# Keys and values of a gated linear attention turned by VectorE in 32 by 32 blocks and gathered by DMAs, in place of TensorE transposes

## The chip, the cores and the metric

The kernel runs on one core of a Trainium2 chip. The metric is the device time of one execution in microseconds (us). Engines are named as in the profile: PE (TensorE), DVE (VectorE), ACT (ScalarE), POOL (GpSimd) and SP (SyncE), which here issues DMAs.

## What is computed

One inference step of a decoder with two layers over 320 tokens: a prompt of 256 and 8 samples of 8 new tokens each. Layer 0 mixes tokens by gated linear attention (GLA), layer 1 by a gMLP with spatial gating; each is followed by a dense MLP of 2048 to 8192 to 2048. The change lies in GLA alone. Cut to that:

```python
D_MODEL = 2048; GLA_HEADS = 4; GLA_HEAD_K = 256; GLA_HEAD_V = 512; GLA_CHUNK = 64

def gla_chunked(q, k, v, log_a, s0):              # one head: q, k (T, 256), v (T, 512)
    def step(s, inp):
        qi, ki, vi, gi = inp                      # a chunk of at most 64 tokens
        b = jnp.cumsum(gi, axis=-2)
        b_last = b[..., -1:, :]
        q_dec = qi * jnp.exp(b)
        k_inv = ki * jnp.exp(-b)
        k_to_end = ki * jnp.exp(b_last - b)
        scores = jnp.where(causal, jnp.einsum('bhtk,bhsk->bhts', q_dec, k_inv), 0.0)
        o = (jnp.einsum('bhtk,bhkv->bhtv', q_dec, s)
             + jnp.einsum('bhts,bhsv->bhtv', scores, vi))
        s_new = (jnp.exp(b_last[..., 0, :])[..., None] * s
                 + jnp.einsum('bhsk,bhsv->bhkv', k_to_end, vi))
        return s_new, o

def gla_mixer(x, w_in, w_gate, b_gate, norm_g, w_out, s0):
    q, k, v, r, g_low = split(x @ w_in)
    log_a = log_sigmoid(g_low @ w_gate + b_gate) / 16
    o, s_fin = gla_chunked(q, k, v, log_a, s0)
    o = o * rsqrt(mean(o * o) + 1e-6) * norm_g    # per head
    return (o * silu(r)) @ w_out, s_fin
```

The prompt starts from a zero state, each sample from a state of its own that is loaded from memory and written back.

## The kernel before

**Tokens lie along the free axis.** A projection leaves features on the 128 partitions and the 320 tokens in the columns (0 to 255 prompt, 256 to 319 samples). Scores are computed from that layout. Three products need keys or values with tokens on the partitions instead: the outputs from the scores (`prompt_o`, `sample_first`), the prompt's final state (`prompt_state`) and the samples' state updates (`sample_step`). So keys and values are turned: `ev_k` and `ev_v`, called as the projection of 128 key or value features ends, do it.

**Weights.** Every weight matrix is cut into units of 512 rows and 256 columns. `unit()` has SP load one into `raw` (L138, 512 KB, three buffers), ACT cast it to a rounded high part `wh` (L144) and DVE subtract to get the low part `wl` (L145); `wh` and `wl` have four buffers each until `second_half()`, a second set after it. TensorE multiplies a unit in 24 matmuls: for each of 4 blocks of rows and 2 of columns wl by x_high, wh by x_low, wh by x_high (L161 to L163). `group()` runs 4 units for 256 output columns, or 8 for two such blocks that share the inputs, and then calls the evictions. Units are counted here in the order in which TensorE uses them: head 0 uses units 1 to 8 for V, 9 to 16 for K and Q, 17 to 24 for the gate R; heads 1 to 3 use, from 24h + 1 on, 8 for K and Q, 8 for V (two groups of 4) and 8 for R. The output projection `gla_w_out` starts at unit 97.

**Side work.** A `Side` object holds a list of steps and runs some of them after each unit: gates of the next head, and the attention steps of a head (`Head.steps`) during its R units and the next head's K, Q units. The steps are written in program order, but the order on each engine is set when the program is built, by a scheduler with its own estimate of when inputs are ready; so an instruction may stand far from where it was written. An engine then runs its list strictly in order. SP's list holds the loads of weights and of sample states (`load`, L578), and each DMA of it uses one of eight completion counters in turn, so that a DMA waits for the one eight places before.

**The turn before.** `ev_k` prepares two tiles of 128 features by 256: `kend` (prompt) and `kst` (samples, 32 columns for each, high and low part), `ev_v` likewise `vfm` and `vst`. Each is transposed on TensorE in two blocks of 128 by 128 into PSUM (L420, L422, L456, L458) and copied from there by ACT or DVE: to `ktp` (L424), `kz` (L429, L431: each sample's keys alone, zeros around them), `vtp` (L460), `vts` (L461).

**Buffers.** Pool `g3` has four buffers of 512 KB under the tag "st", in which the states of the samples and the prompt's new state turn; `gp` has one buffer to a tag, `g2` two. `gltile()` gives one of four PSUM tiles. At the end of a head `sample_o` turns the samples' outputs back (L615), sums squares over features by a matmul with ones (L625), and `rsqrt` (L186 to L190) makes the norm's factor.

Of the kernel before, what the change touches and what calls it, by code (L numbers as in the profile page):

```python
# [8 lines left out]
F32 = mybir.dt.float32  # L9
F32R = mybir.dt.float32r  # L10
# [5 lines left out]
P = 128  # L16
# [61 lines left out]
def step_kernel(ctx: ExitStack, tc: tile.TileContext, A):  # L78
# [3 lines left out]
    def nm(s):  # L82
        uid[0] += 1
        return f"{s}_{uid[0]}"
# [22 lines left out]
    def gltile(n=512):  # L107
        return gl.tile([P, n], F32, tag="gl", name=nm("gl"), padded_shape=[P, 512])
# [173 lines left out]

    kz = gp.tile([P, 2, 4, DK], F32R, tag="kz", name="kz")
    nc.gpsimd.memset(kz[:].bitcast(F32), 0.0)
# [6 lines left out]
    def load_gates():  # L291

        nc.sync.dma_start(wgr, A["gla_w_low"])
        wgr2 = gp.tile([P, 2, DV], F32, tag="vtp", name="wgr2")[:].rearrange("p a b -> p (a b)")
        for i in range(6):
            nc.sync.dma_start(wgr2[16 * i : 16 * (i + 1), :], A["gla_w_gate"])
        nc.scalar.copy(wg2[:], wgr2[0:96])
        nc.vector.tensor_sub(wg2[64:96, :], wgr2[64:96], wg2[64:96, :].bitcast(F32))
# [25 lines left out]
    def bc4(ap):  # L324

        return ap.rearrange("p (b o t) -> p b o t", b=DB, o=1)

    def chunks(ap):
        return ap.rearrange("p (n w) -> p n w", w=CH)

    class Head:
# [58 lines left out]
        def factors(hd):  # L390
# [6 lines left out]
            nc.vector.tensor_mul(fac[:, :, 5:6], fac[:, :, 2:3], d3)  # L397

        def ev_k(hd, kt, ps):
            ei, ee = hd.ei[kt], hd.ee[kt]  # L400
# [15 lines left out]
            nc.vector.tensor_sub(kst[:, :, 2:4, :], bc4(kte[:, TP:T]).to_broadcast(two), hi)  # L416
            pt = gltile()
            ks = kst[:].rearrange("p b c t -> p (b c t)")
            for blk in range(2):
                nc.tensor.transpose(pt[:, blk * P : (blk + 1) * P], kend[:, blk * P : (blk + 1) * P], ident[:])  # L420
            for g in range(2):
                nc.tensor.transpose(pt[:, TP + g * P : TP + (g + 1) * P], ks[:, g * P : (g + 1) * P], ident[:])  # L422
            cs = slice(kt * P, (kt + 1) * P)
            nc.scalar.copy(hd.ktp[:, :, cs], pt[:, 0:TP].rearrange("p (b f) -> p b f", f=P))  # L424
            for i in range(4):
                rows = slice(32 * i, 32 * (i + 1))
                src = pt[rows, TP:].rearrange("p (b f) -> p b f", f=P)
                if i % 2:
                    nc.scalar.copy(kz[rows, :, i, cs], src)  # L429
                else:  # L430
                    nc.vector.tensor_copy(kz[rows, :, i, cs], src)  # L431

# [12 lines left out]
        def ev_v(hd, vt, ps):  # L445
            vfm = g2.tile([P, TP], F32, tag="vfm", name=nm("vfm"))
            nc.scalar.copy(vfm[:], ps[:, 0:TP])
            vst = g2.tile([P, DB, 4, DS], F32, tag="vst", name=nm("vst"))
            two = [P, DB, 2, DS]
            hi = vst[:, :, 0::2, :]  # L450
            nc.scalar.copy(hi.bitcast(F32R), bc4(ps[:, TP:T]).to_broadcast(two))
            nc.vector.tensor_sub(vst[:, :, 1::2, :], bc4(ps[:, TP:T]).to_broadcast(two), hi)
            pt = gltile()
            vs = vst[:].rearrange("p b c t -> p (b c t)")
            for blk in range(2):
                nc.tensor.transpose(pt[:, blk * P : (blk + 1) * P], vfm[:, blk * P : (blk + 1) * P], ident[:])  # L456
            for g in range(2):
                nc.tensor.transpose(pt[:, TP + g * P : TP + (g + 1) * P], vs[:, g * P : (g + 1) * P], ident[:])  # L458
            cs = slice(vt * P, (vt + 1) * P)
            nc.scalar.copy(hd.vtp[:, :, cs], pt[:, 0:TP].rearrange("p (b f) -> p b f", f=P))  # L460
            nc.vector.tensor_copy(hd.vts[:, :, cs], pt[:, TP:].rearrange("p (b f) -> p b f", f=P))  # L461

# [70 lines left out]
        def prompt_o(hd, i):  # L533
# [6 lines left out]
            for v in range(2):  # L540
                vs = slice((2 * i + v) * P, (2 * i + v + 1) * P)
                nc.tensor.matmul(pv[:, v, :], hd.vtp[:, 0, vs], scp[:, 0:W0], start=(v == 0), stop=False)  # L542
                nc.tensor.matmul(pv[:, v, P:TP], hd.vtp[:, 1, vs], scp[:, W0:], start=False, stop=(v == 1))  # L543
            nc.scalar.copy(o_all[:, 4 * h + 2 * i : 4 * h + 2 * i + 2, 0:TP], pv)
# [8 lines left out]
        def prompt_state(hd, kt):  # L553
            if kt == 0:
                hd.S = g3.tile([P, 2, DV], F32, tag="st", name=nm("S"))
            pu = gltile()
            for blk in range(2):
                nc.tensor.matmul(pu[:], hd.ktp[:, blk, kt * P : (kt + 1) * P], hd.vtp[:, blk, :],  # L558
                                 start=(blk == 0), stop=(blk == 1))
# [20 lines left out]
        def sample_first(hd):  # L580

            hd.st = {}
            hd.load(0)
            hd.load(1)
            hd.po = gltile()
            for g in range(2):
                nc.tensor.matmul(hd.po[:], scst[:, g, :], hd.vts[:, g, :], start=(g == 0), stop=False)

        def sample_step(hd, b, kt):
# [12 lines left out]
            pu = gltile()  # L602
            nc.tensor.matmul(pu[:], kz[:, g, i, kt * P : (kt + 1) * P], hd.vts[:, g, :], start=True, stop=True)  # L603
            nc.vector.scalar_tensor_tensor(st[:, kt, :], st[:, kt, :], hd.dec[:, kt, NCH + b : NCH + b + 1],
# [500 lines left out]
```

## Time and profile before

| | |
|---|---|
| median of 3 runs | 2703.79 us (2703.7 to 2705.22) |
| the profiled execution | 2703.75 us |
| its span in the profile | 2702.0 us |
| mean granted TensorE clock | 0.999 |
| PE, DVE, ACT, POOL busy | 2692.4, 1543.5, 1182.8, 53.5 us |
| DMA | 434.53 MB, mean 161 GB/s |

The profile shows one execution. Its span runs from the first to the last instruction, and the time of the execution is 1.75 us longer. A busy time is the union of an engine's instructions; matmuls overlap, so the sum of their durations is more than what they take of the span. Line numbers are those of each kernel's own file: a line of the kernel before that lies behind the change stands 16 to 19 lines further down in the changed one (L600 becomes L616, L615 L631, L625 L641; L569 and L521 become L588 and L537).

### The profile page before, as it was taken

The page shows a single profiled execution, that of the slowest core. Times are in us where ns is not written, and L with a number is a line of the kernel's source. Part 1 is how long each engine was busy: PE and PEld are TensorE (multiplying, and loading weights), DVE is VectorE, ACT ScalarE, POOL GpSimd, SP SyncE. Part 2 cuts the span into 40 slices and gives each one's busy share as a digit, 9 for nine tenths or more (in the row PEclk, how much of TensorE's full clock was granted, in tenths as well). Part 3 has the DMA queues.
Part 4 walks back from the last instruction along what each step waited for, and adds up shares of the span by engine and source line. Part 5 has one row for each costly group of instructions (what it writes and reads, how often), then busy time and mean ns, then how long its engine had stood idle before and what let it go on. Part 6 is the DMA issues. An engine that isn't in the chain of part 4 may idle for free.

```text
span 2702.0 us, 44679 instructions
## 1 busy us (share of the span) xinstructions
PE 2692.4 (100%) x18515; PEld 2669.7 (99%) x18515; DVE 1543.5 (57%) x2289; ACT 1182.8 (44%) x1702; POOL 53.5 (2%) x83
## 2 busy tenths in 40 slices
PE   9999999999999999999999999999999999999998
PEld 9999999999999999999999999999999999999998
DVE  6667577885444444444468775587444444444456
ACT  6545455464234334333445554355334323333434
POOL 1000001000000000000001000000000000000000
PEclk9999999999999999999999999999999999999999
DMA  7656556644445455444445444454444545554442
GB/s 243 193 188 228 185 190 218 211 146 156 152 151 154 151 154 151 153 151 153 150 148 171 150 140 136 140 162 155 150 155 150 154 151 153 152 153 152 153 152 79
DMA packets 126396, 434.53 MB, mean 161 GB/s; under 512 B 13680, under 2 KB 17904, under 8 KB 126192
## 3 DMA queue, kind: packets, MB, share of 16 engines
q1 hardware_dynamic: 119136, 407.82, 48.6%
q0 software_dynamic: 6512, 23.20, 2.6%
q8 instruction: 145, 2.38, 0.4%
q10 hardware_dynamic: 544, 0.66, 0.1%
q14 instruction: 59, 0.48, 0.1%
HBM read 409.60 MB, written 22.02 MB: 160 GB/s over the span
## 4 chain that ended last, share of the span: by engine, by line
PE 99%; ACT 0%; DMA 0%; DVE 0%; issue 0%; ACTq 0%; DVEq 0%
PE mm L161 32%; PE mm L163 31%; PE mm L162 31%; PE gl L600 1%; PE gl L603 1%; PE gl L558 1%; PE gl L948 0%; PE gl L542 0%; DMA raw<-gla_w_in 0%; ACT z L1038 0%; PE gl L943 0%; DMA xr<-xT 0%; PE gl L543 0%; PE gl L458 0%; PE gl L456 0%; PE gl L521 0%
## 5 line engine op out<-in xcount | busy, mean ns | idle before, releaser
L145 DVE TENSOR_TENSOR wl<-raw,wh 128x1024 fp32r<-128x1024 f32 (+1 forms) x740 | 901.6, 1219 | 938.8 <-ACT wh L144 936.3
L144 ACT CAST wh<-raw 128x1024 fp32r<-128x1024 f32 (+1 forms) x740 | 771.3, 1044 | 1201.3 <-PE mm L163 1080.9
L163 PE MATMUL mm<-yh,wh 128*128 128x320 f32 x2624 | 805.0, 307 | 0.0
L161 PE MATMUL mm<-yh,wl 128*128 128x320 f32 x2624 | 803.1, 308 | 0.0
L162 PE MATMUL mm<-yl,wh 128*128 128x320 f32 x2624 | 794.2, 303 | 0.0
L161 PE MATMUL mm<-hh,wl 128*128 128x320 f32 x2048 | 630.8, 308 | 0.0
L163 PE MATMUL mm<-hh,wh 128*128 128x320 f32 x2048 | 628.7, 307 | 0.0
L162 PE MATMUL mm<-hl,wh 128*128 128x320 f32 x2048 | 619.6, 303 | 0.0
L162 PEld LDWEIGHTS mm<-yl,wh 128*128 128x128 f32 x2624 | 492.5, 188 | 0.0
L161 PEld LDWEIGHTS mm<-yh,wl 128*128 128x128 f32 x2624 | 490.9, 188 | 0.0
L163 PEld LDWEIGHTS mm<-yh,wh 128*128 128x128 f32 x2624 | 490.8, 187 | 0.0
L162 PEld LDWEIGHTS mm<-hl,wh 128*128 128x128 f32 x2048 | 384.4, 188 | 0.0
L161 PEld LDWEIGHTS mm<-hh,wl 128*128 128x128 f32 x2048 | 384.4, 188 | 0.0
L163 PEld LDWEIGHTS mm<-hh,wh 128*128 128x128 f32 x2048 | 383.0, 187 | 0.0
L161 PE MATMUL mm<-xh,wl 128*128 128x320 f32 x768 | 241.1, 314 | 0.9 <-DVE wl L145 0.5
L163 PE MATMUL mm<-xh,wh 128*128 128x320 f32 x768 | 236.7, 308 | 0.0
L162 PE MATMUL mm<-xl,wh 128*128 128x320 f32 x768 | 234.7, 306 | 0.0
L161 PEld LDWEIGHTS mm<-xh,wl 128*128 128x128 f32 x768 | 144.1, 188 | 5.4 <-issue 1.9
L162 PEld LDWEIGHTS mm<-xl,wh 128*128 128x128 f32 x768 | 144.3, 188 | 3.5 <-issue 1.2
L163 PEld LDWEIGHTS mm<-xh,wh 128*128 128x128 f32 x768 | 143.9, 187 | 1.3
L857 DVE TENSOR_TENSOR hl<-f,hh 128x320 fp32r<-128x320 f32 x128 | 62.3, 489 | 29.4 <-ACT hh L856 29.4
L161 PE MATMUL mm<-oh,wl 128*128 128x320 f32 x256 | 78.1, 309 | 0.6 <-DVE nw L187 0.6
(268 smaller groups left out, 2112.2 us busy)
## 6 DMA issues: line engine op xcount, KB each, us to landing
raw<-mlp_w SPq DMA_DIRECT2D x512, 512.0 KB, 3.5
raw<-gla_w_in SPq DMA_DIRECT2D x94, 512.0 KB, 4.2
raw<-sg_w_in SPq DMA_DIRECT2D x64, 512.0 KB, 3.5
st<-state SPq DMA_DIRECT2D x32, 512.0 KB, 4.3
o_state_s<-st POOLq DMA_DIRECT2D x32, 512.0 KB, 3.8
raw<-gla_w_out SPq DMA_DIRECT2D x32, 512.0 KB, 4.2
raw<-sg_w_out SPq DMA_DIRECT2D x32, 512.0 KB, 3.5
z<-xT POOLq DMA_DIRECT2D x2, 1280.0 KB, 11.6
```

The lines of the kernel that those rows point to most:

```text
L144: nc.scalar.copy(hi[:, ks, :], raw[:, ks, :])
L145: nc.vector.tensor_sub(lo[:, ks, :], raw[:, ks, :], hi[:, ks, :].bitcast(F32))
L161: nc.tensor.matmul(ps, wl[:, kk, s], x_h, start=first, stop=False)
L162: nc.tensor.matmul(ps, wh[:, kk, s], x_l, start=False, stop=False)
L163: nc.tensor.matmul(ps, wh[:, kk, s], x_h, start=False, stop=last)
L558: nc.tensor.matmul(pu[:], hd.ktp[:, blk, kt * P : (kt + 1) * P], hd.vtp[:, blk, :], start=(blk == 0), stop=(blk == 1))
L600: nc.tensor.matmul(po[:], qm[:, kt, b * P : (b + 1) * P], part[:], start=False, stop=(b == DB - 1 and kt == 1 and part is sth))
L603: nc.tensor.matmul(pu[:], kz[:, g, i, kt * P : (kt + 1) * P], hd.vts[:, g, :], start=True, stop=True)
L857: nc.vector.tensor_sub(hl[:, j, 0:T], f[:], hh[:, j, 0:T].bitcast(F32))
```

## The change

Keys and values are turned in two steps. DVE turns each 32 by 32 block of a 128 by 256 tile in place (`nc.vector.transpose`, 48 of them: 16 for keys, 32 for values) into a tile `blk` of pool `g3`; values come straight from PSUM. Then DMAs on SP's queue move blocks to their rows: `gather` issues four DMAs, each from 32 partitions to 32 others in runs of 32 numbers (128 bytes). A head issues 32 DMAs of keys (32 x 4 x 32 numbers, 16 KB each) and, for each half of the values, 16 (32 x 8 x 32 numbers, 32 KB each): 256 DMAs in all. `kz` and the new `ktp` and `va` (in place of `vtp` and `vts`) have layouts in which a gather writes whole runs, and the readers' views follow (`vt_prompt`, `v_prompt`, `v_sample`, `pairs`). The 96 transposes on TensorE and the 72 copies out of PSUM are gone, the 16 to `vfm` too. Two steps are also written in another place: the loads of a head's first two states stand in `sample_scores` and no longer in `sample_first`, and `prompt_scores` stands ahead of `sample_first`. The diff, without the readers whose views alone change:

```diff
-    kz = gp.tile([P, 2, 4, DK], F32R, tag="kz", name="kz")
+    kz = gp.tile([P, 4, 2, 2, P], F32R, tag="kz", name="kz")
...
-            hd.ktp = gp.tile([P, 2, DK], F32, tag="ktp", name=nm("ktp"))
-            hd.vtp = gp.tile([P, 2, DV], F32, tag="vtp", name=nm("vtp"))
-            hd.vts = gp.tile([P, 2, DV], F32R, tag="vts", name=nm("vts"))
+            hd.ktp = gp.tile([P, 2, 2, P], F32, tag="ktp", name=nm("ktp"))
+            hd.va = gp.tile([P, 2, 2, 2, 2, P], F32, tag="vtp", name=nm("va"))
...
+        def blocks(hd):
+            return g3.tile([P, 4, TP], F32, tag="st", name=nm("blk"))
+
+        def gather(hd, dst, blk, q):
+            n = blk.shape[1] // P
+            src = blk.rearrange("p (n q f) -> p n q f", q=4, f=32)
+            out = dst.rearrange("p (n i f) -> p n i f", i=4, f=32)
+            for i in range(4):
+                nc.sync.dma_start(out[32 * q : 32 * (q + 1), :, i, :], src[32 * i : 32 * (i + 1), :, q, :])
...
         def ev_k(hd, kt, ps):
...
-            pt = gltile()
-            ks = kst[:].rearrange("p b c t -> p (b c t)")
-            for blk in range(2):
-                nc.tensor.transpose(pt[:, blk * P : (blk + 1) * P], kend[:, blk * P : (blk + 1) * P], ident[:])
-            for g in range(2):
-                nc.tensor.transpose(pt[:, TP + g * P : TP + (g + 1) * P], ks[:, g * P : (g + 1) * P], ident[:])
-            cs = slice(kt * P, (kt + 1) * P)
-            nc.scalar.copy(hd.ktp[:, :, cs], pt[:, 0:TP].rearrange("p (b f) -> p b f", f=P))
-            for i in range(4):
-                rows = slice(32 * i, 32 * (i + 1))
-                src = pt[rows, TP:].rearrange("p (b f) -> p b f", f=P)
-                if i % 2:
-                    nc.scalar.copy(kz[rows, :, i, cs], src)
-                else:
-                    nc.vector.tensor_copy(kz[rows, :, i, cs], src)
+            if kt == 0:
+                hd.kb = hd.blocks()
+            nc.vector.transpose(hd.kb[:, kt, :], kend[:])
+            nc.vector.transpose(hd.kb[:, 2 + kt, :], kst[:].rearrange("p b c t -> p (b c t)"))
+            if kt == 1:
+                kb = hd.kb[:].rearrange("p a b -> p (a b)")
+                for q in range(4):
+                    hd.gather(hd.ktp[:].rearrange("p k b f -> p (k b f)"), kb[:, 0 : 2 * TP], q)
+                    hd.gather(kz[:, q].bitcast(F32).rearrange("p k b f -> p (k b f)"), kb[:, 2 * TP :], q)
...
         def ev_v(hd, vt, ps):
-            vfm = g2.tile([P, TP], F32, tag="vfm", name=nm("vfm"))
-            nc.scalar.copy(vfm[:], ps[:, 0:TP])
+            if vt % 2 == 0:
+                hd.vb = hd.blocks()
+            nc.vector.transpose(hd.vb[:, vt % 2, :], ps[:, 0:TP])
...
-            (two pairs of transposes and two copies, as in ev_k)
+            nc.vector.transpose(hd.vb[:, 2 + vt % 2, :], vst[:].rearrange("p b c t -> p (b c t)"))
+            if vt % 2:
+                for q in range(4):
+                    hd.gather(hd.va[:, vt // 2].rearrange("p c v b f -> p (c v b f)"),
+                              hd.vb[:].rearrange("p a b -> p (a b)"), q)
...
         def sample_scores(hd):
+            hd.st = {}
+            hd.load(0)
+            hd.load(1)
...
         def sample_first(hd):
-            hd.st = {}
-            hd.load(0)
-            hd.load(1)
...
             yield hd.sample_scores
+            yield hd.prompt_scores
             yield hd.sample_first
...
-            prompt = [hd.prompt_scores, lambda: hd.prompt_o(0), lambda: hd.prompt_o(1),
+            prompt = [lambda: hd.prompt_o(0), lambda: hd.prompt_o(1),
```

The scheduler's order of the changed program differs in places that the diff does not show. Below, a row is an instruction with its line, operation and operands; numbers behind a name tell one tile from another, and "x5" counts equal rows that follow each other.

SP before, head 1 (`raw_1830` is unit 36, and the loads of `raw` below it units 37 to 41):

```order
L578 DMA st_2129<-state 128x2x512
L138 DMA raw_1830<-gla_w_in 128x1024
L578 DMA st_2220<-state 128x2x512
L138 DMA raw_1886<-gla_w_in 128x1024
L138 DMA raw_1916<-gla_w_in 128x1024
L138 DMA raw_1946<-gla_w_in 128x1024
L138 DMA raw_1976<-gla_w_in 128x1024
L138 DMA raw_2032<-gla_w_in 128x1024
```

Loads of weights follow each other here. SP of the changed kernel at the same place (`raw_1927` is unit 37, `raw_1957` unit 38, `raw_1987` unit 39):

```order
L138 DMA raw_1927<-gla_w_in 128x1024
L138 DMA raw_1957<-gla_w_in 128x1024
L422 DMA kz<-blk_1721 32x4x32 x5
L422 DMA ktp_1711<-blk_1721 32x4x32 x8
L422 DMA kz<-blk_1721 32x4x32 x3
L422 DMA ktp_1711<-blk_1721 32x4x32 x4
L422 DMA kz<-blk_1721 32x4x32 x4
L422 DMA ktp_1711<-blk_1721 32x4x32 x4
L422 DMA kz<-blk_1721 32x4x32 x4
L422 DMA va_1712<-blk_1898 32x8x32 x16
L138 DMA raw_1987<-gla_w_in 128x1024
```

Between the loads of units 38 and 39 now stand 48 gathers, all keys of head 1 and the first half of its values. In heads 2 and 3 the same block stands ahead of the loads of units 63 and 87. The second half of the values (16) follows the load of unit 47 (71, 95). In head 0, 32 gathers of values stand ahead of the load of unit 15 and 32 of keys behind that of unit 22.

DVE of the changed kernel where those values are turned (`wl_1959` is unit 38; the rows of L188 to L528 belong to the norm of head 0):

```order
L145 TENSOR_TENSOR wl_1959<-raw_1957,wh_1958 128x1024
L188 TENSOR_TENSOR nw_1631<-nw_1631,ny_1632 128x320
L189 TENSOR_TENSOR nw_1631<-nw_1631,ny_1632 128x320
L190 SCALAR_TENSOR_TENSOR rs_1630<-nw_1631,ny_1632 128x320
L528 TENSOR_TENSOR o_all_91<-o_all_91,rs_1630 128x320 x4
L467 STREAM_TRANSPOSE blk_1898<-mm_1776 128x256
L467 STREAM_TRANSPOSE blk_1898<-mm_1777 128x256
L472 TENSOR_TENSOR vst_1900<-mm_1776,vst_1900 128x16x8
L473 STREAM_TRANSPOSE blk_1898<-vst_1900 128x256
L472 TENSOR_TENSOR vst_1905<-mm_1777,vst_1905 128x16x8
L473 STREAM_TRANSPOSE blk_1898<-vst_1905 128x256
```

The values `mm_1776` and `mm_1777` are finished by TensorE with unit 36. On TensorE the scores of head 1, L588, L537 and L543, now stand behind the last matmul of unit 38 (of units 62 and 86 in heads 2 and 3); before, they stood behind units 41 and 42.

PE before, in the output projection's first group (`sample_o` of head 3; L615 turns the outputs, and L625, the sum, follows 35 rows later, again between matmuls):

```order
L161 MATMUL mm_4804<-oh_4799,wl_4953 128x320
L162 MATMUL mm_4804<-ol_4800,wh_4952 128x320
L615 MATMUL gl_4855<-ident,os_4853 128x128 x4
L163 MATMUL mm_4804<-oh_4799,wh_4952 128x320
L161 MATMUL mm_4804<-oh_4799,wl_4953 128x320
```

PE of the changed kernel, the same steps (L616 are the last samples' outputs, L631 the turn, L641 the sum; `wl_5250` is unit 103):

```order
L163 MATMUL mm_4892<-oh_4887,wh_5108 128x320
L616 MATMUL gl_4480<-stl_4875,qm 128x512
L616 MATMUL gl_4480<-sth_4874,qm 128x512
L616 MATMUL gl_4480<-stl_4932,qm 128x512
L616 MATMUL gl_4480<-sth_4931,qm 128x512
L631 MATMUL gl_4943<-ident,os_4941 128x128 x4
L641 MATMUL gl_4953<-s_691_4513,ones 128x320
L161 MATMUL mm_5246<-oh_4887,wl_5250 128x320
L162 MATMUL mm_5246<-ol_4888,wh_5249 128x320
```

The outputs, the turn and the sum of head 3 now stand together between two units.

More of the change, by code (lines that the diff above doesn't have):

```diff
@@ L293, in load_gates @@
         nc.sync.dma_start(wgr, A["gla_w_low"])
-        wgr2 = gp.tile([P, 2, DV], F32, tag="vtp", name="wgr2")[:].rearrange("p a b -> p (a b)")
+        wgr2 = gp.tile([P, 4, DV], F32, tag="vtp", name="wgr2")[:].rearrange("p a b -> p (a b)")[:, 0 : H * DK]
         for i in range(6):
@@ L326, in bc4, with pairs @@
         return ap.rearrange("p (b o t) -> p b o t", b=DB, o=1)
+    def pairs(t):
+        return t[:].rearrange("p (a v f) -> p a v f", a=2, v=2)
     def chunks(ap):
@@ L452, in ev_v @@
             nc.vector.tensor_sub(vst[:, :, 1::2, :], bc4(ps[:, TP:T]).to_broadcast(two), hi)
[L453 to L461, printed above, removed]
+            nc.vector.transpose(hd.vb[:, 2 + vt % 2, :], vst[:].rearrange("p b c t -> p (b c t)"))
[3 more added lines that the diff above has]
+                              hd.vb[:].rearrange("p a b -> p (a b)"), q)
         def project_kq(hd, side):
@@ L540, in prompt_o @@
             for v in range(2):
-                vs = slice((2 * i + v) * P, (2 * i + v + 1) * P)
-                nc.tensor.matmul(pv[:, v, :], hd.vtp[:, 0, vs], scp[:, 0:W0], start=(v == 0), stop=False)
-                nc.tensor.matmul(pv[:, v, P:TP], hd.vtp[:, 1, vs], scp[:, W0:], start=False, stop=(v == 1))
+                vt = 2 * i + v
+                nc.tensor.matmul(pv[:, v, :], hd.vt_prompt(vt, 0), scp[:, 0:W0], start=(v == 0), stop=False)
+                nc.tensor.matmul(pv[:, v, P:TP], hd.vt_prompt(vt, 1), scp[:, W0:], start=False, stop=(v == 1))
             nc.scalar.copy(o_all[:, 4 * h + 2 * i : 4 * h + 2 * i + 2, 0:TP], pv)
@@ L557, in prompt_state @@
             for blk in range(2):
-                nc.tensor.matmul(pu[:], hd.ktp[:, blk, kt * P : (kt + 1) * P], hd.vtp[:, blk, :],
+                nc.tensor.matmul(pairs(pu), hd.ktp[:, kt, blk, :], hd.v_prompt(blk),
                                  start=(blk == 0), stop=(blk == 1))
@@ L580, in sample_first @@
         def sample_first(hd):
-            hd.st = {}
-            hd.load(0)
-            hd.load(1)
             hd.po = gltile()
             for g in range(2):
-                nc.tensor.matmul(hd.po[:], scst[:, g, :], hd.vts[:, g, :], start=(g == 0), stop=False)
+                nc.tensor.matmul(pairs(hd.po), scst[:, g, :], hd.v_sample(g), start=(g == 0), stop=False)
         def sample_step(hd, b, kt):
@@ L602, in sample_step @@
             pu = gltile()
-            nc.tensor.matmul(pu[:], kz[:, g, i, kt * P : (kt + 1) * P], hd.vts[:, g, :], start=True, stop=True)
+            nc.tensor.matmul(pairs(pu), kz[:, i, kt, g, :], hd.v_sample(g), start=True, stop=True)
             nc.vector.scalar_tensor_tensor(st[:, kt, :], st[:, kt, :], hd.dec[:, kt, NCH + b : NCH + b + 1],
```

6 lines of the change are left out of this document (added).

## The prediction

> **What bounds the kernel now.** I read the engines' busy time, the chain that ended last and the waits first, then the timeline around one head. TensorE is busy for 2692.4 of 2702.0 us, and it is the whole chain.
>
> ```profile
> PE 2692.4 (100%) x18515; PEld 2669.7 (99%) x18515; DVE 1543.5 (57%) x2289; ACT 1182.8 (44%) x1702; POOL 53.5 (2%) x83
> ...
> PE 99%; ACT 0%; DMA 0%; DVE 0%; issue 0%; ACTq 0%; DVEq 0%
> ```
>
> So TensorE work that goes is time saved, and any gap that opens on TensorE is time lost; DVE and ACT have room. What keeps the gaps away is the supply of weights, seen in the waits:
>
> ```profile
> ACT wh L144 <- PE mm L163: 1080.9, 487, 3.1
> SPq L138 <- DVE wl L145: 2148.8, 694, 8.9
> PE mm L161 <- DVE nw L187: 0.6, 1, 0.6
> ```
>
> ACT's cast of a weight unit waits until TensorE gives a buffer back, SP's load waits until DVE has cast the unit that held the raw buffer: the supply runs ahead by all of its buffers. TensorE waits once, 0.6 us, at the end of the GLA part. The cover is countable. There are four cast units and three raw ones, and the casts of head 1 follow TensorE unit by unit:
>
> ```profile
> 166.67 1.05 ACT L144 CAST wh<-raw 128x1024 fp32r<-128x1024 f32 x1
> 170.13 1.05 ACT L144 CAST wh<-raw 128x1024 fp32r<-128x1024 f32 x1 [2.41 <-PE mm L163]
> 171.22 1.23 DVE L145 TENSOR_TENSOR wl<-raw,wh 128x1024 fp32r<-128x1024 f32 x1 [2.24 <-ACT wh L144]
> ```
>
> One unit is 24 matmuls and lasts 170.13 - 166.67 = 3.46 us. When SP sends the load of unit n+7, TensorE has just finished unit n. If SP is then held up, TensorE still has units n+1 to n+6.
>
> **Removed: 96 transposes on TensorE.**
>
> ```profile
> L456 PE MATMUL gl<-ident,vfm 128*128 128x128 f32 x32 | 6.2, 271 | 0.0
> L458 PE MATMUL gl<-ident,vst 128*128 128x128 f32 x32 | 6.1, 272 | 0.0
> L422 PE MATMUL gl<-ident,kst 128*128 128x128 f32 x16 | 3.1, 272 | 0.0
> L420 PE MATMUL gl<-ident,kend 128*128 128x128 f32 x16 | 3.0, 271 | 0.0
> ```
>
> These 271 ns overlap the neighbours. What a pair costs is read from the starts:
>
> ```profile
> 163.35 0.31 PE L161 MATMUL mm<-xh,wl 128*128 128x320 f32 x1
> 163.50 0.31 PE L162 MATMUL mm<-xl,wh 128*128 128x320 f32 x1
> 163.65 0.38 PE L456 MATMUL gl<-ident,vfm 128*128 128x128 f32 x2
> 163.78 0.39 PE L163 MATMUL mm<-xh,wh 128*128 128x320 f32 x1
> 164.01 0.31 PE L161 MATMUL mm<-xh,wl 128*128 128x320 f32 x1
> ```
>
> From L162 to the next L161 there are 0.51 us; two steps of 0.145 would be 0.29, so a pair costs 0.22 us. 48 pairs by 0.22 = 10.6 us, all on the path. Gain: 10.6 us.
>
> The Trainium skill ("TensorE: Matmul & The Clock Gate", Part 4: PE-mode transpose) gives about 275 ns for a transpose in a kernel. The duration here, 271 ns, agrees with it, but the starts do not charge it. By that figure the gain would be estimated at 96 x 0.275 = 26.4 us, 15.8 us more than I take, and the sum at 2704.
>
> **Moved between DVE and ACT.** DVE gets 48 block transposes and loses 16 casts of L461 and 16 of L431; ACT loses 56 copies. No block transpose is in the trace; the nearest row, with the same 128x256 elements out of PSUM, is L461.
>
> ```profile
> L461 DVE CAST vts<-gl x16: 397/425/426, 42.7 to 397.2; 128x256 fp32r<-128x256 f32 x16
> L431 DVE CAST kz<-gl x16: 402/416/423, 71.6 to 374.7; 32x256 fp32r<-32x256 f32 x16
> ```
>
> At 0.42 each DVE gains 48 x 0.42 - 32 x 0.42 = 6.7 us of work over four heads (none at all to 20 if a block transpose took between 0.28 and 0.7). It is off the path, hidden under TensorE's 3.46 us units; where the cover ends it counts, in the chain below.
>
> **Added: 256 gathers on SP.** Each head issues 32 of keys (16 KB, 128-byte runs) and 32 of values (32 KB), in the queue that loads the weights. Eight DMAs of this queue can be open: each gather waits for the one eight before. Their pace g is not in the trace. The issue rows and the smallest transfers bound it:
>
> ```profile
> L296 SPq DMA_DIRECT2D wgr<-gla_w_gate x6: 311/311/420, 7.4 to 14.0; - x6
> L578 SPq DMA_DIRECT2D st<-state x32: 368/379/427, 22.5 to 434.3; - x32
> L138 SPq DMA_DIRECT2D raw<-mlp_w x512: 327/328/328, 525.6 to 2651.0; - x171
> DMA to landing us min/median/max: 3.3/3.5/10.3
> bsp<-sg_wT POOLq DMA_DIRECT2D x8, 2.0 KB, 5.4
> DMA to landing us min/median/max: 2.9/5.4/6.0
> ```
>
> Low end: issue alone, 0.31 us. High end: eight per landing of the 2 KB transfers (short runs too), (5.4 + 0.33)/8 = 0.72 us. With the 2.9 us of that row's quickest, (2.9 + 0.33)/8 = 0.40. I take 0.45, near 0.40, since no weight load is in flight beside the gathers, with a little for the short runs.
>
> *Heads 1 to 3, the large block.* The order puts 32 gathers of keys and 16 of values between the loads of units 38 and 39 of head 1 (and the like of heads 2, 3). Zero is the end of unit 32, where the projections of K and Q end. Keys: five of kz go before; the others follow one cast, one wl and five short DVE operations, some 4 us, then 27 by 0.45, done at 16. Values: TensorE ends unit 36 at 4 x 3.46 + 0.4 (L625) = 14.2, DVE then has two block transposes more than it could do before, two subtractions and one more, about 1.9 us:
>
> ```profile
> 160.78 0.27 ACT L451 CAST vst<-mm 128x128 fp32r<-128x128 f32 x1
> 161.53 0.29 DVE L452 TENSOR_TENSOR vst<-mm,vst 128x128 f32<-128x128 f32 x1
> ```
>
> So they start at 16.1 whatever the keys did, and take 16 x 0.45 = 7.2. The load of unit 39 then leaves SP at 23.6, lands at 27.1 (3.5), and is cast by 29.4 (1.05 + 1.23). TensorE wants it at 14.2 + 2 x 3.46 + the scores that now stand there:
>
> ```profile
> 181.20 0.97 PE L569 MATMUL gl<-qd,kis 128*128 128x32 f32 x8
> 182.01 0.39 PE L161 MATMUL mm<-xh,wl 128*128 128x320 f32 x1
> 187.30 0.34 PE L521 MATMUL gl<-qd,kip 128*64 128x64 f32 x4
> ...
> 188.79 0.51 PE L600 MATMUL gl<-stl,qm 128*128 128x512 f32 x1
> ```
>
> 0.81 + 1.49 = 2.3, so at 23.4. Gap: 6.0 us, three times: 18 us. At 0.31 it is 3.8 (three: 11), at 0.72 17 (keys then last to 23.5 and push the values: three: 52). Behind the stalled load, ACT and DVE wait in order for unit 39, but nothing that TensorE needs earlier. The second block of values (16) stands later, after the load of unit 47; its first reader comes some 20 us after its transposes may start, against 7 of gathers and a few of queueing: no cost.
>
> *Head 0.* 32 gathers of values stand before the load of unit 15. Zero is the end of unit 8. They start at 1.3 (three block transposes), end at 1.3 + 32 x 0.45 = 15.7, and unit 15 is ready at 15.7 + 5.8 = 21.5, wanted at 6 x 3.46 + 0.3 = 21.1. Gap: 0.4; nothing at 0.31, 9 at 0.72. Its keys stand before the load of unit 23, six units after their projection; scores, states and outputs stand between those units as well, and their first reader waits for a quarter of the keys alone: hidden.
>
> *Loads of states.* The first two of a head now stand with the scores, behind the load of unit 45 and far ahead of their readers: two issues by 0.38, hidden by a supply that is by then full again.
>
> *The tail of head 3.* The heads' steps are pulled back by the gathers, and the order now ends them late: sums of the last head (L641) directly behind its transposes (L631), and the next unit of weights directly behind L641. Before, other units stood between.
>
> ```profile
> 451.84 0.59 ACT L612 COPY os<-gl 128x512 f32<-128x512 f32 x1 [2.77 <-PE gl L600]
> 455.12 0.60 PE L615 MATMUL gl<-ident,os 128*128 128x128 f32 x4
> 455.76 0.37 ACT L618 COPY o_all<-gl 128x256 f32<-128x256 f32 x1 [2.23 <-PE gl L615]
> 457.07 0.62 DVE L622 TENSOR_REDUCE s<-sq 128x64 f32<-128x256 f32 x1 [0.48 <-ACT sq L621]
> 463.28 0.53 ACT L186 ACTIVATE ny<-gl,eps_h 128x320 f32<-128x320 f32 x1
> 467.04 0.49 DVE L190 SCALAR_TENSOR_TENSOR rs<-nw,ny 128x320 f32<-128x320 f32 x1
> ```
>
> TensorE idles for the copy (0.6), from L618 to the end of L622 (457.69 - 455.76 = 1.9), and then for ny (0.5), two casts (2.1) or, beside them on DVE, L188, L189, wl, L190 and the wl of its own unit (the two wl 2.5): 4.8. That is 7.3, and about 1 more where the first matmuls of the last quarter wait for the split of head 3; less the 0.6 of before, 8 us. Low end 4 (if the casts come first), high end 12.
>
> **The sum.** The profiled execution took 2703.75 us (span 2702.0), against a median of 2703.79: no difference. 2703.75 - 10.6 + 18 + 0.4 + 8 = 2719.5, say 2719.
>
> The Trainium skill ("DMA: Bandwidth & Descriptors", Rules for kernel authors) says to join many small transfers, since under 64 KB mostly overhead is paid, and (Anatomy of one DMA) puts that at about 2.0 us each. Eight open would then give an estimate of (2.0 + 0.33)/8 = 0.29, SP's issue would bind at 0.33, and the sum would be 2703.75 - 10.6 + 12 + 8 = 2713. No run here shows a transfer of 128-byte runs.
>
> **Rivals.** A difference under 0.2% (5.4 us) of this kernel can hardly be told from none.
>
> 1. *Hidden gathers* (faster). The gathers leave before their turn is needed, the gap at unit 39 is nil, the tail costs little. For it: DMA queues have room, the supply of weights waits in 2148.8 us of rows. It decides if values start and pass in 23.4 - 6.1 - 16.1 = 1.2 us, 0.08 us a gather; SP's quickest issue is 0.31. 2703.75 - 10.6 = 2693. Chance 0.07.
> 2. *A draw.* g at its low end and a tail of 4: 2703.75 - 10.6 + 11 + 4 = 2708; or the transposes were dearer than their starts show, near their full rows (6.2 + 6.1 + 3.1 + 3.0 = 18.4): 2703.75 - 18.4 + 18 + 8 = 2711, just outside the draw, and a draw only with the low end of the gathers (2704). The starts speak against it: 0.03. Chance 0.15 for both. The Trainium skill's figure, quoted above, is the rule behind this second case.
> 3. *Slow short runs.* The sixteen engines need as long for a gather as the high end: gaps of 17 three times, 9 in head 0, tail 8: 2703.75 - 10.6 + 52 + 9 + 8 = 2762. For it: the 5.4 us of a 2 KB transfer; against it: that row had megabytes beside it. Chance 0.2 for above 2740.
>
> The forecast, gaps that outweigh the gain, has 0.58. Slower by over 0.2% (above 2709): 0.58 + 0.2 = 0.78; within: 0.15; faster: 0.07. The range goes from the tail of rival 2, 2703, to the lower part of rival 3, 2750.
>
> **What would show it.** TensorE's busy time falls by some 10 us; its waits list the wl of a gla_w_in unit three times, 4 to 9 us each, and one sum (L641) and one weight wait near 440 to 460 us; the gathers stand on SP in rows of 48 lasting 17 to 25 us. The forecast is wrong if SP passes gathers quicker than weight loads, or much slower than 0.7, or if VectorE's block transposes take over 1 us, when the values would start later.

## The result, and the profile after

The changed kernel takes 2778.47 us (median of 6 runs, 2776.05 to 2779.27), against 2704.79 for the kernel before beside it: a ratio of 1.0271 [1.0258, 1.0284]. It is 73.7 us slower, where 15 were forecast, and the time lies above the range. The profiled execution took 2776.05 us, with a span of 2774.0, which is 72.0 longer than before.

The page, engines and clock first, then the chain that ended last:

```profile
PE 2691.5 (97%) x18419; PEld 2668.5 (96%) x18419; DVE 1549.2 (56%) x2305; ACT 1165.6 (42%) x1646; POOL 53.5 (2%) x83
...
PE   8979797899999999999999999999999999999999
...
PEclk9989898999999999999999999999999999999999
...
PE 93%; SPq 3%; DMA 2%; DVE 1%; ACT 1%; issue 1%; ACTq 0%; DVEq 0%
```

TensorE's busy time hardly moved (2692.4 before), though it executes 96 instructions fewer. Its idle time went from 9.6 to 82.5 us, 72.9 more, as much as the whole loss. The idle time lies almost wholly in the first eight of the 40 slices, in which the granted clock falls too. SP's queue, which was nowhere on the chain, now makes 3% of it. The waits on TensorE:

```profile
PE mm L161 <- DVE wl L145: 70.5, 6, 20.4
PE gl L641 <- DVE s L638: 2.1, 1, 2.1
PE gl L616 <- DVE stl L614: 1.5, 1, 1.5
```

Columns: waits in total, how many, the longest. Five of the six waits for `wl` are waits for a unit of `gla_w_in`: 7.10 us in head 0, 18.92, 18.94 and 20.43 in heads 1 to 3, and the sixth, 4.87, is the tail in `gla_w_out`; the remainder is small. The waits in heads 0, 2 and 3 (head 1 follows below):

```profile
67.77 0.63 PE L161 MATMUL mm<-xh,wl 128*128 128x320 f32 x1 [7.10 <-DVE wl L145]
323.58 0.63 PE L161 MATMUL mm<-xh,wl 128*128 128x320 f32 x1 [18.94 <-DVE wl L145]
450.77 0.64 PE L161 MATMUL mm<-xh,wl 128*128 128x320 f32 x1 [20.43 <-DVE wl L145]
```

`wl` is only the last link. SP's timeline in head 1 (start, duration of the row, what, how many) shows what held it:

```profile
159.78 3.18 SPq L422 DMA_DIRECT2D kz<-blk  x5
163.05 5.10 SPq L422 DMA_DIRECT2D ktp<-blk  x8
...
177.96 3.49 SPq L422 DMA_DIRECT2D kz<-blk  x4
181.56 10.46 SPq L422 DMA_DIRECT2D va<-blk  x16
192.12 12.56 SPq L138 DMA_DIRECT2D raw<-gla_w_in  x7
```

The 48 gathers follow each other without a pause, from 159.78 to 192.12, 32.3 us or 0.67 each, and only then does the next load of weights go out. The values were turned by 172.0, but their gathers had to stand behind the keys until 181.56. The other engines from the moment of that load:

```profile
196.01 1.04 ACT L144 CAST wh<-raw 128x1024 fp32r<-128x1024 f32 x1 [17.57 <-DMA raw<-gla_w_in]
197.09 1.23 DVE L145 TENSOR_TENSOR wl<-raw,wh 128x1024 fp32r<-128x1024 f32 x1 [16.49 <-ACT wh L144]
...
198.37 0.64 PE L161 MATMUL mm<-xh,wl 128*128 128x320 f32 x1 [18.92 <-DVE wl L145]
198.80 0.47 PE L162 MATMUL mm<-xl,wh 128*128 128x320 f32 x1
199.07 0.47 PE L163 MATMUL mm<-xh,wh 128*128 128x320 f32 x1
```

ACT had waited 17.57 us for the data, DVE 16.49 for ACT, TensorE 18.92 for DVE: one delay seen on three engines. The next question is whether the gathers were slow to issue or slow to land. Answer of the trace on their line (name and count, then min/median/max in ns; between them stands ktp with the same 599):

```profile
L422 SPq DMA_DIRECT2D va<-blk x128: 585/609/1576, 39.1 to 474.7; - x128
...
L422 SPq DMA_DIRECT2D kz<-blk x64: 585/599/1649, 81.4 to 433.0; - x64
DMA to landing us min/median/max: 1.8/1.9/5.4
```

They land in 1.9 us, so in the time of one landing SP issues three: eight completion counters cannot bind here. The 16 DMA engines were busy for 17 to 30% of the time between 160 and 192. What takes the time is SP itself, 0.6 us to issue each, nearly twice as long as for a load of weights that stands alone (0.33).

### The profile page after: what moved, and what is told of

Read it like the earlier page. It is cut to its first block, busy times and chain, and to the rows that moved or that the text cites. A ratio compares the mean times of both kernels' runs of the same rounds, so it can differ in the third digit from the quotient of the medians.

```text
span 2774.0 us, 44762 instructions
## 1 busy us (share of the span) xinstructions
PE 2691.5 (97%) x18419; PEld 2668.5 (96%) x18419; DVE 1549.2 (56%) x2305; ACT 1165.6 (42%) x1646; POOL 53.5 (2%) x83
## 4 chain that ended last, share of the span: by engine, by line
PE 93%; SPq 3%; DMA 2%; DVE 1%; ACT 1%; issue 1%; ACTq 0%; DVEq 0%
PE mm L161 30%; PE mm L163 30%; PE mm L162 29%; SPq L422 3%; DMA raw<-gla_w_in 1%; PE gl L616 1%; PE gl L619 0%; DVE wl L145 0%; PE gl L574 0%; ACT wh L144 0%; PE gl L965 0%; DMA o_state_s<-st 0%; ACT z L1055 0%; DMA st<-state 0%; PE gl L960 0%
## 5 line engine op out<-in xcount | busy, mean ns | idle before, releaser
L163 PE MATMUL mm<-oh,wh 128*128 128x320 f32 x256 | 79.1, 310 | 0.0
```

What stands on the lines that cost most here:

```text
L163: nc.tensor.matmul(ps, wh[:, kk, s], x_h, start=False, stop=last)
```

## The experiments

Three theories stood after the result. T1: SP's issue of the gathers holds up the loads of weights, and nothing else of the change costs anything. T2: the gathers cost wherever they are issued. T3: the order and the layout that came with them cost. And inside T1: the issue is slow because of the gathers' shape, or because of the place they stand at.

**The order and the layout alone (e_pe_all).** The changed kernel's step order and its layout of the keys, but keys and values turned by TensorE as before.

```diff
-            nc.vector.transpose(hd.kb[:, kt, :], kend[:])
...
+                nc.tensor.transpose(pt[:, blk * P : (blk + 1) * P], kend[:, blk * P : (blk + 1) * P], ident[:])
...
```

> The changed kernel's order of steps (state loads with the scores, prompt scores ahead of the first sample product) and its layouts of keys, but all keys and values turned by TensorE again; no gather, no block transpose. Theory 1: as before the change, 2704 within 3. A third theory, that the reordered steps and layouts cost part of the loss themselves: 2710 to 2740.

2703.75 us, ratio 0.9999 [0.999, 1.0009]. The written order and the layout cost nothing; the whole loss is in the turn.

**The other queue (e_pool).** One word: the 256 gathers are issued by POOL.

```diff
-                nc.sync.dma_start(out[32 * q : 32 * (q + 1), :, i, :], src[32 * i : 32 * (i + 1), :, q, :])
+                nc.gpsimd.dma_start(out[32 * q : 32 * (q + 1), :, i, :], src[32 * i : 32 * (i + 1), :, q, :])
```

> The changed kernel with its 256 gathers issued by POOL and no longer by SP; nothing else is written differently. Theory 1 (the gathers hold up the weight loads that stand behind them in SP's queue): the waits for wl in head 0 and at units 39, 63 and 87 (7.1, 18.9, 18.9, 20.4 us) are gone, with the slow matmuls behind them; the tail of head 3 stays, since its order is the same. 2704 - 10.6 + 9.5 = 2703, between 2697 and 2710. Theory 2 (the gathers' traffic in short runs, or the later block transposes, make keys, values and weights late, whichever queue issues): the waits stay, 2760 to 2780.

2735.98 us, ratio 1.0118 [1.0103, 1.0133]: neither. The waits on TensorE:

```profile
PE gl L616 <- DVE stl L614: 7.6, 6, 3.4
PE gl L619 <- DVE st L620: 6.1, 2, 3.1
PE mm L161 <- DVE qd L454: 5.7, 2, 2.9
PE mm L161 <- DVE wl L145: 4.9, 2, 4.3
```

No wait for `gla_w_in` is left but 0.55 us near the start (of the 4.9 for `wl`, 4.35 is the tail, in `gla_w_out`): taken off SP, the gathers hold up no weights. That part of T1 is shown. But 42 us of the 73.7 came back, not all, so something else costs too. TensorE is idle for 25.8 us more than in the kernel before, and its busy time is 17.2 above that of e_none, which executes the same matmuls (2698.9 against 2681.7); less the 10.7 of the transposes, that is the 32.3 by which the span is still longer. The waits are now those of the samples' steps (L616, L619) for DVE. In this program the scheduler put the first product with gathered values in head 1 behind 54.7 units, 42.3 before and 45.5 in the changed kernel; the steps that follow then stand one behind another on TensorE at the end of the head, with no unit between them while DVE updates a state. That the late first product causes the bunching is read from the order, not shown by this run. The gathers themselves also behave differently here: on POOL their issue takes 0.55 to 0.58 us, and they land after 3.5 to 4.2 us (medians by tile), where those from SP landed after 1.8 to 2.0.

**Keys alone (e_keys), values alone (e_values).** Each keeps the other's turn on TensorE; the gathers of what is turned stay on SP. The line that goes in e_keys, and the one in e_values:

```diff
-            nc.vector.transpose(hd.vb[:, vt % 2, :], ps[:, 0:TP])
...
-            nc.vector.transpose(hd.kb[:, kt, :], kend[:])
...
```

> Keys alone are turned by VectorE and gathered on SP (128 gathers); values go through TensorE. Theory 1: no wait in head 0; in heads 1 to 3, 32 gathers ahead of the load of unit 39 (63, 87) start 3.8 us after the K and Q projections and last 20.8, the weights come at 30.9, wanted at about 23.4: 7.5 us, with 1.25 of slow matmuls; 32 transposes gone. 2704 - 3.5 + 3 x 8.8 = 2727, between 2715 and 2740. Theory 2 (traffic): half of the loss, 2742.

> Values alone are turned by VectorE and gathered on SP (128 gathers); keys go through TensorE. Theory 1: head 0 keeps its wait of 7.1 us (32 gathers ahead of the load of unit 15). In heads 1 to 3 two blocks of 16 stand ahead of the load of unit 44; the first ends early, the second starts about 2 us after unit 40 and lasts 16 x 0.65 = 10.4, so the weights come 2 + 10.4 + 6.3 = 18.7 after unit 40, wanted at 3 x 3.46 + 2.3 = 12.7: 6 us each. With 1.25 us of slow matmuls for each wait and 64 of the 96 transposes gone: 2704 - 7.1 + 8.4 + 3 x 7.3 = 2727, between 2715 and 2740. Theory 2 (traffic): half of the loss, 2742.

Keys alone: 2736.93 us, 1.0125 [1.0108, 1.0142], 10 above what was expected (though inside the range): the three waits are 9.3 us in place of 7.5, and TensorE's busy time (2697.7) lies 9 us above that of e_none with two thirds of the transposes left in (both priced below), 3 us for each wait where 1.25 of slow matmuls were expected. Values alone: 2726.62, 1.0082 [1.0067, 1.0097], as expected in sum, but with other waits than expected, so the agreement is luck. First e_keys, then e_values:

```profile
PE mm L161 <- DVE wl L145: 27.9, 4, 9.3
```

```profile
PE mm L161 <- DVE wl L145: 13.2, 3, 7.6
PE gl L608 <- DMA va<-blk: 8.6, 3, 2.9
```

In e_keys TensorE waits 9.26, 9.34 and 9.12 us for the unit behind 32 gathers. The full change has 48 gathers at that place and waits 18.92 in head 1. (18.9 - 9.3) / 16 = 0.60 us for each gather more: the wait grows by the issue time of a gather, which is what T1 says and what a fixed cost of the block would not give. In e_values the values wait for no keys, the loads of weights keep up in heads 1 to 3, and TensorE waits for the gathers themselves, 2.9 us a head; in head 0 the 32 gathers of values stand as in the full change, and the wait there is 7.62 (7.10 in the full change).

**Gathers on ACT (e_act).** `nc.scalar.dma_start` in the same line.

> The changed kernel with its gathers issued by ACT. Theory 1, in the form that whatever stands behind the gathers waits: not the loads but the casts of weights (L144) wait now. In heads 1 to 3, 32 gathers stand ahead of the cast of unit 40: 1 + 20.8 + 1 us against 13.8 of TensorE's work in hand, about 10 us of wait and 3 of slow matmuls each; head 0 about 5; tail 5. 2704 - 10.6 + 39 + 11 = 2744, between 2725 and 2765. Were it SP alone that issues slowly, 2697 to 2705.

2787.14 us, 1.0309 [1.0295, 1.0324], the worst of all, and outside what was expected. Waits on TensorE, then the gathers' rows:

```profile
PE mm L161 <- DVE wl L145: 41.7, 10, 8.7
PE gl L603 <- DMA va<-blk: 16.0, 3, 6.4
PE gl L603 <- issue: 8.0, 1, 8.0
```

```profile
L422 ACTq DMA_DIRECT2D va<-blk x128: 592/622/1623, 39.1 to 482.7; - x128
```

The issue takes 0.62 us on ACT as well: with the 0.55 to 0.58 on POOL, the price is not one of SP alone. ACT pays it in the engine that casts the weights, so units come late and values too. The wait of 8.0 at L603, in head 0, stands as "issue" because the profile shows nothing that released it.

**No turn at all (e_none).** The kernel before without its 96 transposes; the copies read the untransposed tiles.

```diff
-                nc.tensor.transpose(pt[:, blk * P : (blk + 1) * P], vfm[:, blk * P : (blk + 1) * P], ident[:])
...
-            nc.scalar.copy(hd.vtp[:, :, cs], pt[:, 0:TP].rearrange("p (b f) -> p b f", f=P))
+            nc.scalar.copy(hd.vtp[:, :, cs], vfm[:, 0:TP].rearrange("p (b f) -> p b f", f=P))
...
```

> The kernel before with the 96 TensorE transposes left out: the same copies of ACT and DVE read the tiles untransposed. It prices what the change removes. By the spacing of the starts (0.22 us a pair): 2704 - 10.6 = 2693, between 2691 and 2696. By the durations of their rows (18.4 to 26 us): 2678 to 2686.

2691.9 us, 0.9956 [0.9944, 0.9969]: 12.0 us for 96 transposes, 0.125 each, and TensorE's busy time falls by 10.7:

```profile
PE 2681.7 (100%) x18419; PEld 2659.3 (99%) x18419; DVE 1540.3 (57%) x2289; ACT 1182.6 (44%) x1702; POOL 53.6 (2%) x83
```

TensorE is the whole chain, so turning keys and values elsewhere can hardly gain more in this kernel than these 12 us. The run also measures a second loss: the changed kernel executes the same 18419 matmuls in 2691.5 us, 9.8 more. Most of that are matmuls at half clock, below.

**Both queues, a better order (e_mixf).** Keys and the first half of the values on POOL, the second half on SP (in head 0 all on POOL), and the first product with values held at 44 units (68 and 91 in heads 2 and 3): five empty steps ahead of it set the place, and the next weight matmul is made to follow it on TensorE.

```diff
-                                hd.vb[:].rearrange("p a b -> p (a b)"), q)
+                                hd.vb[:].rearrange("p a b -> p (a b)"), q, nc.sync if vt == 3 and hd.h else nc.gpsimd)
...
+                last[0] = nc.tensor.matmul(pairs(hd.po), scst[:, g, :], hd.v_sample(g), start=(g == 0), stop=False)
...
```

> Gathers off the path as far as I can put them: keys and the first half of the values issued by POOL, the second half by SP behind the load of unit 47 (head 0 by POOL alone); and TensorE's order held, so that the first product with gathered values stands at 44.0 units (68, 91) and not where the scheduler would put it. Theory 1 (what is lost is the queue in front of the weights, and the order behind it): no wait for wl in heads 0 to 3, a tail of 4 to 8 us: 2697 to 2702. Theory 2 (traffic or late block transposes): over 2730.

2716.79 us, 1.0049 [1.0035, 1.0063]: 15 to 20 us above what was expected.

```profile
PE gl L607 <- DMA va<-blk: 8.0, 3, 4.7
PE mm L162 <- DVE wl L146: 5.2, 3, 4.6
PE gl L620 <- DVE stl L618: 2.6, 2, 1.7
```

The bunched steps of e_pool are gone (7.6 and 6.1 there, 2.6 here), but now the values land after TensorE asks for them. With the early order the gathers are too late, with the late one the steps stand together.

**Keys alone, on POOL (e_kpool).**

> The part of the change that should be free, by theory 1: keys alone by VectorE and gathers, issued by POOL; values through TensorE, and with them the order of the kernel before (the first product of gathered keys with values stands at 42.0 units). 32 of 96 transposes gone, no wait: 2704 - 3.9 = 2700, between 2698 and 2703 (by the measured price of the transposes, 12 us for 96, a third is 4). If the traffic or the block transposes cost something themselves: 2704 or more.

2703.57 us, 0.9999 [0.9989, 1.0008]: a draw, without the gain of 4 that was expected. The 32 transposes of the keys are gone, and one new wait of 2.0 us (L619 for `stl`) is there. This is the best way of the change that was found, and it gains nothing that can be told from zero.

**What a gather's issue costs, and why (e_forms, e_forms2, e_forms3).** More DMAs on SP at the end of the kernel before, four or six of each form; each kernel was executed once. In e_forms they follow each other at once:

> The kernel before, with 32 more DMAs on SP at its end, four of each of eight forms, for their issue times (gathers took 0.60 us, weight loads 0.33). In order of lines: 32 partitions x 4 x 128 bytes between tiles (as a gather of keys), 32 x 8 x 128 bytes (as values), 32 x 512 bytes whole, 32 x 128 bytes, 32 x 4 x 128 bytes from memory, 32 x 2048 bytes whole, 128 x 2 x 128 bytes, 128 x 1024 bytes whole. If short runs set the issue time, the whole ones take 0.33 and all others 0.60; if the number of runs, it rises from 0.3 (32 runs) to 0.6 (256); if a source in SBUF, all take 0.60 but the one from memory; if 32 partitions, the last two take 0.33 and the first six 0.60.

All eight, from 32 runs of 128 bytes to 128 rows of 1 KB, took 0.588 to 0.638 us (medians): sent like this, shape and size tell nothing. One of the eight came from memory (0.598, in four runs a row), the rest from a tile. In e_forms2 a load of weights takes turns with a gather:

> The kernel before, with more DMAs on SP at its end, to find what makes a gather's issue 0.60 us and a weight load's 0.33: 128 x 4 KB whole rows from memory (a weight load), the same from a tile to a tile, 32 x 2 KB from memory, 128 x 1 KB pieces from memory, 128 x 256 bytes from memory; then a gather of keys and a weight load in turn, each waiting for the landing of the one before of its kind. If the length of a row sets it: 0.33, 0.33, 0.38, 0.49, 0.60. If a tile as source sets it: 0.60 for the second and the gathers alone. If it is the closeness of one DMA to the next: weight loads take 0.60 here too, and both less where they wait in turn.

```profile
L1061 SPq DMA_DIRECT2D z<-z x6: 597/598/725, 2714.1 to 2730.0; - x6
...
L1063 SPq DMA_DIRECT2D z<-mlp_w x6: 336/337/588, 2714.9 to 2733.2; - x6
```

The gather takes 0.60 though a load stands ahead of it: it is not another gather ahead that makes it dear. The loads took 0.34 where SP had stood still for 1.7 us or more before them, but the one that followed a gather at once, at 2714.89, took the 0.59. In the changed kernel too, three loads that follow each other at 192.12 take 1.49 us together, 0.50 each. So 0.33 is the price of a load that stands alone. The other five forms of e_forms2 went out partly close together and partly among the kernel's last stores; they scatter from 0.34 to 1.37 us and decide nothing. In e_forms3 each DMA waits for the landing of the one before, so that nothing queues:

> The kernel before, with 32 DMAs on SP at its end, each waiting for the landing of the one before, so that none is close to another. In order of lines, four of each: 32 x 4 x 128 bytes tile to tile (a gather of keys), the same from memory, 32 x 512 bytes tile to tile, the same from memory, 128 x 512 bytes tile to tile, 128 x 4 KB tile to tile, the same from memory (a weight load), 32 x 4 KB from memory. If a tile as source makes the issue slow: 0.60 for forms 1, 3, 5, 6 and 0.34 for the others. If runs of 128 bytes do: 0.60 for the first two, 0.34 for the rest. If 32 partitions do: 0.60 for 1 to 4 and 8.

```profile
L1052 SPq DMA_DIRECT2D z<-z x4: 586/606/837, 2697.3 to 2704.0; - x4
L1054 SPq DMA_DIRECT2D z<-state x4: 564/570/602, 2705.9 to 2712.4; - x4
L1056 SPq DMA_DIRECT2D z<-z x4: 507/526/577, 2714.3 to 2719.6; - x4
L1058 SPq DMA_DIRECT2D z<-state x4: 310/322/356, 2721.3 to 2726.0; - x4
L1060 SPq DMA_DIRECT2D z<-z x4: 465/486/525, 2727.6 to 2733.2; - x4
L1062 SPq DMA_DIRECT2D z<-z x4: 465/465/465, 2735.0 to 2743.7; - x4
L1064 SPq DMA_DIRECT2D z<-mlp_w x4: 328/342/357, 2746.6 to 2757.1; - x4
L1066 SPq DMA_DIRECT2D z<-mlp_w x4: 310/318/327, 2760.5 to 2767.3; - x4
```

In pairs: L1052 is a gather of keys (32 rows, four runs of 128 bytes, tile to tile), L1054 the same from memory; L1056 is one run of 512 bytes to each of 32 rows, tile to tile, L1058 the same from memory; L1060 and L1062 are 128 rows of 512 bytes and of 4 KB, tile to tile; L1064 is a load of weights, L1066 a quarter of one on 32 rows. From memory in whole rows an issue takes 0.32 to 0.34, whether 16 KB or 512 KB; tile to tile 0.47 to 0.53; in four runs a row 0.57 to 0.61 from either. Standing alone, bytes and rows make little difference, the source and the runs do. Why, and why forms with whole rows cost 0.59 to 0.60 when they follow each other at once (L1055 and L1065 of e_forms), no run here tells.

## Why the prediction was wrong, point by point

**Right.** The mechanism, its places and the sign: gathers in the queue of the weights, three waits of `wl` in heads 1 to 3, one in head 0, and a tail behind L631 and L641. The block transposes on DVE, guessed at 0.42 us from a cast:

```profile
L467 DVE STREAM_TRANSPOSE blk<-mm 128x256 f32<-128x256 f32 x16 | 7.1, 443 | 3.4 <-PE mm L163 3.3
L473 DVE STREAM_TRANSPOSE blk<-vst 128x256 f32<-128x256 f32 x16 | 6.9, 433 | 0.3
```

They take 0.44, are done at 172.0, which is 16.0 after unit 32 (16.1 predicted), and no wait of TensorE is put down to them. TensorE stopped at 179.45, 23.4 after the end of unit 32 near 156.0, exactly when it was said to want unit 39. The tail:

```profile
526.52 0.66 PE L631 MATMUL gl<-ident,os 128*128 128x128 f32 x4 [0.68 <-ACT os L628]
529.26 1.41 PE L641 MATMUL gl<-s,ones 128*128 128x320 f32 x2 [2.08 <-DVE s L638]
535.54 0.64 PE L161 MATMUL mm<-oh,wl 128*128 128x320 f32 x1 [4.87 <-DVE wl L145]
```

0.7, 2.1 and 4.9, against 0.6, 1.9 and 4.8.

**The removed transposes.** 10.6 predicted, 10.7 of TensorE's busy time and 12.0 of the whole measured by e_none. The starts were the right view, not the rows of 271 ns. The Trainium skill's figure in "TensorE: Matmul & The Clock Gate" (Part 4: PE-mode transpose), about 275 ns, by which the gain was put at 26.4, is the duration of one, and e_none shows that this is not its price between other matmuls.

**The step that failed: the pace g.** It was bounded from below by the issue of whole rows from memory (0.31) and from above by landings (0.72), and 0.45 was taken "near 0.40, since no weight load is in flight". The view was that landings set the pace, and that an issue costs the same whatever it moves. Both halves were off: landings bind nothing (1.9 us against eight issues of 0.6), and the issue of a gather, 0.6, is nearly twice that of a load that stands alone. The row taken for the low end had another source and other runs than the DMA it stood for, and went out with room before it (six in 6.6 us). The prediction's other estimate, 2713 from landings of 2.0 us, had the landings about right (1.8 to 2.0 here) and failed at the same step. 0.67 lay within the bounds, near the upper end, so the terms of the upper end were the right ones for another reason.

**A second step, smaller.** "Five of kz go before" the zero, the end of unit 32. They left SP at 159.78, 3.8 after it: these gathers read both blocks of sample keys, and DVE began to turn the second only at 159.28 (the first at 153.10), behind the four products of the norm that had become ready (L522, 156.29 to 158.15), two `qd` and a block of prompt keys. With all 48 gathers behind that point the prediction's own scheme gives 3.8 + 32.3 + 6.25 (landing 3.9, two casts) - 23.4 = 18.9, the wait that was measured; with five ahead it would have been 27 by 0.67 + 16 by 0.67 from 4.0, a gap of 15.7.

**A missing term: the clock.** Busy times and the granted clock (PEclk) in head 1; the columns are stretch, length, then busy time of PE, PEld, DVE, ACT and POOL, PEclk, DMA share, GB/s:

```profile
180.00:184.00 4.00, 0.00 (x0) 0.00 (x0) 0.58 (x3) 0.00 (x0) 0.00 (x0) 1.00 0.21 31
184.00:185.00 1.00, 0.00 (x0) 0.00 (x0) 0.00 (x0) 0.00 (x0) 0.00 (x0) 0.59 0.36 48
185.00:198.00 13.00, 0.00 (x0) 0.00 (x0) 0.91 (x1) 1.64 (x2) 0.00 (x0) 0.50 0.53 152
198.00:201.00 3.00, 2.63 (x10) 2.63 (x11) 2.77 (x3) 1.50 (x2) 0.00 (x0) 0.50 0.46 139
...
202.00:206.00 4.00, 4.00 (x29) 4.00 (x29) 1.68 (x2) 2.11 (x2) 0.00 (x0) 1.00 0.69 251
```

Some 5 us after TensorE stopped, the clock is halved, and it comes back 3 us after the restart. Until then matmuls start 0.27 us apart (198.80, 199.07) and not 0.145. A wait costs more than its length; over the whole kernel that is most of the 9.8 us between e_none's busy time and this one's: of the first 560 us, in stretches of 1 us, those with a granted clock below 0.9 hold 20.4 us of TensorE's busy time here and none in e_none, and the clock's shortfall times the busy time adds up to 9.4 us. The Trainium skill ("TensorE: Matmul & The Clock Gate", Part 1: The HAM clock gate) puts the default clock at half, after an idle window of about 3.4 us, and the return at about 3.4 us of work; the trace agrees roughly, with 5 and 3 us. The prediction has no term for it; before the change the clock was 0.999 throughout.

**The sum as it came out.** What went: 10.7 of transposes. What came: 18.9 + 18.9 + 20.4 = 58.3 for the three waits (18 predicted), 7.1 in head 0 (0.4), 7.6 in the tail (8), 1.5 for a sample's state (nothing), 9.8 of slower matmuls, most of it half clock (nothing); less 1.1 of waits of before that are gone. 72.5, against a span longer by 72.0. Head 0 follows the pace as well: 1.3 + 32 x 0.67 + 5.8 - 21.1 = 7.4.

**The rivals.** *Hidden gathers* and *a draw* did not come; the draw came with e_kpool, where the gathers leave SP and the values stay on TensorE. *Slow short runs* had the time nearest to it, 2762, for a reason that is not there: the sixteen engines were not slow. It had a chance of 0.2, and the price that decided between it and the forecast was the one that the trace of before did not hold.

## What to carry to other kernels

In these runs a DMA cost its issuing engine time by its form and by what stood just ahead of it, hardly by its bytes. Price many small DMAs by issue time times their number, from a row with the same source, the same runs and as little room before it, and if there is no such row, say that the pace is open instead of taking the cheap one. In a queue that also feeds the bottleneck, count the whole block that stands ahead of the next feed, from the moment when the block's first member may go, against the cover that the buffers give. And where waits open on TensorE that were not there, add the slow matmuls that follow each of them.

## What the hardware showed unexpectedly

- The issue of a DMA that stands alone takes SP 0.32 to 0.34 us for whole rows from memory, 0.47 to 0.53 tile to tile, 0.57 to 0.61 in four runs a row (e_forms3); tile to tile, one behind another, 0.59 to 0.64 whatever the form (e_forms). Gathers took 0.61 to 0.62 on ACT (e_act), 0.55 to 0.58 on POOL (e_pool).
- A 32 KB gather landed after 2.0 us from SP and after 4.3 from POOL, in one and the same run (medians of e_mixf).
- A wait of 4.69 us on TensorE (e_mixf, at 408.92) was followed by matmuls 0.27 us apart until 412.4; one of 1.98 (e_kpool, at 133.92) kept the clock at 1.00.
- A block transpose of 128x256 on DVE takes 0.43 to 0.44 us, from PSUM or SBUF alike; the 48 of them take DVE 21 us, the 256 gathers that bring the blocks to their rows hold SP for some 0.6 us each.
